# Conditioning sums on the vector engine, and the elementwise engines of the expert loops in program order

## The chip, the core and the metric

The kernel runs on one core of a Trainium2 chip. The metric is the device time of one launch in microseconds (us). The five engines of the core run side by side and each takes its instructions in order: TensorE (PE, with its weight loads as PEld), VectorE (DVE), ScalarE (ACT), GpSimd (POOL) and SyncE (SP), which issues most of the DMA loads.

## What is computed

A two-layer diffusion transformer with mixture-of-experts layers, batch 1, in f32: 256 image tokens `x` and 256 context tokens `xc`, width 1024. Cut to what matters here:

```python
def adaln(cond, w_ada, b_ada):                       # six vectors of 1024 per stream and layer
    m = jax.nn.silu(cond) @ w_ada + b_ada
    return jnp.split(m[..., None, :], 6, axis=-1)

def hybrid_layer(x, xc, c, c_ctx, ..., update_ctx):
    sh1, sc1, gt1, sh2, sc2, gt2 = adaln(c, w_ada, b_ada)               # first stream
    sh1c, sc1c, gt1c, sh2c, sc2c, gt2c = adaln(c_ctx, w_ada, b_ada)     # second stream
    h = modulate(rmsnorm(x, g_mix), sh1, sc1)
    hc = modulate(rmsnorm(xc, g_mix), sh1c, sc1c)
    ...                                              # w_in, rotary, retention, gating, w_pa, w_pb, w_out
    x = x + gt1 * token_mix(h @ w_in, ...)
    ...                                              # the same for xc in layer 0 only
    y = hier_moe(...)                                # 32 experts, top 2, silu(x@w1)*(x@w3) @ w2
    x = x + gt2 * y[:256];  xc = xc + gt2c * y[256:]
```

Layer 0 updates both token sets (512 tokens through its experts). Layer 1 updates the image tokens alone (256).

## The kernel before

**Stages.** By the trace, layer 0's token mixing runs from 0 to about 580 us, layer 0's experts to about 1087, layer 1's mixing to about 1420, layer 1's experts to about 1895, and the final norm ends the span at 1905.3. The weights of all 32 experts are streamed in both layers.

**Mixing.** A weight piece of 512 KB is loaded (`raw`), rounded by ACT (L206, `whi`), and DVE subtracts to get the rest (L207, `wlo`). PE then multiplies three times (L245, L246, L247), which makes an f32 product of rounded parts. For each of four heads, q and k are projected, DVE makes two rotary products for each of them (L808 to L810), POOL adds them (L811), ACT rounds the sum (L320), and POOL subtracts (L321). PE's score matmuls (L245 `mm<-u,u`) want the rounded k.

**Conditioning.** `ada_steps(l, v)` makes vector `v` of layer `l` in eight steps, each with one 512 KB unit of `w_ada`. DVE multiplies the unit by a per-partition scalar and adds it to the first stream's sum (L400, a `scalar_tensor_tensor` of 128x1024). For the second stream, ACT scales the unit (L402) and POOL adds it to the sum (L403). Layer 1's vectors 2 to 5 have only the first stream. The steps are a list, `background`. PE's program calls `tick()` at each block of its work; the test there lets a step be put into the program at three of four ticks in layer 0 and at every tick in layer 1. Vectors (0,2) to (0,5), (1,0) and (1,1) are planned for layer 0, and (1,2) to (1,5) for layer 1. After the last step, `finish` sums over partitions on PE and adds the bias on DVE, and POOL sends the vector to memory.

**Order.** PE and SP run their programs as written (L72). DVE, ACT and POOL are ordered by a scheduler, but for regions where `manual_schedule(engines=ENG3)` fixes them to the program's order: the start, the `routing` region from the last mixing pieces on (L895, closed in `after_turn` at the second expert), and the `between` region from one layer to the next.

**Experts.** One expert is `expert(...)`: matmuls with w1 and w3 (L1240), Silu on ACT (L1243), a product on DVE (L1244), four transposes on PE (L1249), a copy of them by ACT (L1251, `hTt`), and the w2 matmuls (L1257). Around them stand side jobs: `quad_block` gathers tokens for the next four experts on PE (L1204), copied by ACT (L1208) every second block; `combine_parts` has small reduces on DVE (L1229); `gated` multiplies on DVE (L1281) and adds on POOL (L1282).

Of the kernel before, what the change touches and what calls it, by code (L numbers as in the profile page):

```python
# [51 lines left out]
def hybrid_kernel(  # L52
# [162 lines left out]
    def tick():  # L215
        ticks[0] += 1
        while deferred and deferred[0][0] <= ticks[0]:
            deferred.pop(0)[1]()
        if background and (layer[0] or ticks[0] % 4):
            background.pop(0)()  # L220
# [162 lines left out]
    def ada_steps(l, v):  # L383
# [4 lines left out]
        def step(k):  # L388
            raw = raws.pop(0)
            if nexts:  # L390
                raws.append(ada_raw(*nexts.pop(0), u4t if ticks[0] < 30 else a4t))
            for i in range(streams):
                if k == 0:
                    acc.append((u4t if ticks[0] < 24 else a4t)((P, 4, 256)))
                if k == 0 and i:
                    S.activation(acc[i], raw, AF.Copy, scale=cst[:, k, i:i + 1])
                elif k == 0:
                    V.tensor_scalar(out=acc[i], in0=raw, scalar1=cst[:, k, i:i + 1], scalar2=None, op0=ALU.mult)
                elif i == 0:
                    V.scalar_tensor_tensor(out=acc[i], in0=raw, scalar=cst[:, k, i:i + 1], in1=acc[i], op0=ALU.mult, op1=ALU.add)  # L400
                else:
                    S.activation(raw, raw, AF.Copy, scale=cst[:, k, i:i + 1])  # L402
                    G.tensor_tensor(out=acc[i], in0=raw, in1=acc[i], op=ALU.add)  # L403
            if k == KD - 1:
                b = ada_bias(l, v)
                defer(2 if ticks[0] < 24 else 1, lambda: finish(b))
# [22 lines left out]
        def columns(r):  # L429
# [5 lines left out]
            if v == 3:  # L435
                defer(1, lambda: router_const(l))
# [17 lines left out]
    ada_planned([(0, v) for v in range(2, 6)] + [(1, 0), (1, 1)])  # L454
# [79 lines left out]
    for l in range(depth):  # L534
# [117 lines left out]
        else:  # L652
# [35 lines left out]
            def ada_rest():  # L688
                ada_planned([(1, v) for v in range(2, 6)])
                raws.append(ada_raw(*nexts.pop(0), a4t))  # L690

            defer(15, ada_rest)
        fj = [(f, hx, 0, nq) for f in range(2)]
# [693 lines left out]
        for e in range(EXPERTS):  # L1387
# [35 lines left out]
            def after_turn(e=e, pr=pr, e2=e2, q=q, e4=e4, half=half, more=more, more4=more4):  # L1423
                if e == 1:
# [3 lines left out]
                    routing.close()  # L1428
# [7 lines left out]
                if not last and e == EXPERTS - 1:  # L1436
                    between.enter_context(tc.manual_schedule(engines=ENG3))
# [28 lines left out]
        if last:  # L1466
            gfin = u4t()
            nc.sync.dma_start(gfin, g_final.partition_broadcast(P))
# [131 lines left out]
```

## Time and profile before

| | |
|---|---|
| median of 3 runs | 1906.25 us (1904.4 to 1906.83) |
| profiled execution | 1907.06 us, of it span 1905.3 us |
| mean granted TensorE clock | 0.981 |
| PE busy | 1808.8 us (95%) |
| DVE, ACT, POOL busy | 911.3 (48%), 630.9 (33%), 529.5 (28%) |
| DMA | 553.48 MB, mean 290 GB/s |

The span is the time from the first to the last instruction; 1.76 us lie around it. PE is busy in nearly all of the span, so time is won or lost only where PE waits, or where its clock is granted at half, or where the loads set the pace of PE. A granted clock of 1.00 is 2.4 GHz and 0.50 is 1.2 GHz.

### The profile page before, as it was taken

To read this page: it belongs to the slowest core of one execution; us is meant where nothing else is said; L and a number is where in the kernel's file an instruction comes from. 1 tells how busy PE (TensorE), PEld (TensorE's weight loads), DVE (VectorE), ACT (ScalarE), POOL (GpSimd) and SP (SyncE) were. 2 spreads that over 40 slices of the span, in tenths; PEclk is the share of its full clock that TensorE was granted. 3 is DMA by queue.
4 is the path that set the end of the run, shared out by engine and by line. 5 is a ranking of instruction groups with operands and counts; after the bars stand their busy time and mean duration, and the time that the engine had idled before them with its cause. 6 is when DMAs were issued, how large, how long until landed. Compare 5 with 4: busy or idle time off the path is not lost. (4 is left out here: it accounts for less than half of the span.)

```text
span 1905.3 us, 28120 instructions
## 1 busy us (share of the span) xinstructions
PE 1808.8 (95%) x10899; PEld 1239.2 (65%) x10899; DVE 911.3 (48%) x1558; ACT 630.9 (33%) x1013; POOL 529.5 (28%) x416
## 2 busy tenths in 40 slices
PE   6999998899998999999999799999989999999996
PEld 5988898798884444444454399999974444444442
DVE  4878575664644323232333378885553222222223
ACT  3635454444333221222121264444432222222222
POOL 1444354432021424242424342132021122122121
PEclk9999998899998999999999999999999999999998
DMA  9445343344777999999999559863798999999995
GB/s 347 126 171 180 128 154 114 100 160 150 205 232 261 394 404 406 404 400 403 407 402 381 195 165 324 273 199 122 231 351 337 409 409 408 409 409 409 409 409 226
DMA packets 234109, 553.48 MB, mean 290 GB/s; under 512 B 23121, under 2 KB 118513, under 8 KB 233970
## 3 DMA queue, kind: packets, MB, share of 16 engines
q1 hardware_dynamic: 233586, 551.57, 77.9%
q8 instruction: 88, 1.44, 0.3%
q14 instruction: 51, 0.42, 0.1%
q0 software_dynamic: 384, 0.05, 0.0%
HBM read 550.45 MB, written 1.10 MB: 289 GB/s over the span
## 5 line engine op out<-in xcount | busy, mean ns | idle before, releaser
L1282 POOL TENSOR_TENSOR u<-u,t 128x512 f32<-128x512 f32 x184 | 236.0, 1319 | 722.8 <-DVE t L1281 722.8
L1240 PE MATMUL mm<-u,a 128*64 128x512 f32 x1376 | 333.6, 592 | 1.9 <-ACT a L1155 1.4
L207 DVE TENSOR_TENSOR wlo<-raw,whi 128x1024 fp32r<-128x1024 f32 x157 | 217.7, 1389 | 154.1 <-ACT whi L206 153.6
L247 PE MATMUL mm<-u,wlo 128*128 128x256 f32 (+1 forms) x800 | 269.5, 337 | 5.4 <-DVE wlo L207 5.4
L245 PE MATMUL mm<-u,whi 128*128 128x256 f32 (+1 forms) x800 | 270.6, 338 | 0.0
L246 PE MATMUL mm<-u,whi 128*128 128x256 f32 (+1 forms) x800 | 268.4, 336 | 0.0
L1267 DVE SCALAR_TENSOR_TENSOR a<-mm,sw,a 64x512 fp32r<-64x512 f32 x128 | 96.0, 750 | 338.5 <-ACT a L1266 338.0
L245 PE MATMUL mm<-whi,u 128*128 128x256 f32 x832 | 240.2, 289 | 1.9 <-ACT u L569 1.5
L247 PE MATMUL mm<-whi,u 128*128 128x256 f32 x832 | 238.0, 286 | 0.7 <-DVE u L571 0.4
L246 PE MATMUL mm<-wlo,u 128*128 128x256 f32 x832 | 237.1, 285 | 0.8 <-DVE wlo L207 0.8
L1240 PEld LDWEIGHTS mm<-u,a 128*64 128x64 f32 x1376 | 106.2, 137 | 196.3 <-issue 177.6
L206 ACT ACTIVATE whi<-raw 128x1024 fp32r<-128x1024 f32 x160 | 169.7, 1063 | 172.3 <-PE mm L246 65.3
L1281 DVE TENSOR_TENSOR t<-mm,u 128x512 f32<-128x512 f32 x190 | 119.5, 676 | 132.4 <-PE mm L1275 131.8
L247 PEld LDWEIGHTS mm<-u,wlo 128*128 128x128 f32 x800 | 152.8, 191 | 22.6 <-DVE wlo L207 7.3
L245 PEld LDWEIGHTS mm<-whi,u 128*128 128x128 f32 x832 | 161.2, 194 | 6.8 <-issue 3.3
L1266 ACT ACTIVATE a<-mm,sw 64x512 fp32r<-64x512 f32 x128 | 87.4, 682 | 232.4 <-PE mm L1257 187.1
L245 PEld LDWEIGHTS mm<-u,whi 128*128 128x128 f32 x800 | 152.9, 191 | 17.4 <-issue 1.6
L247 PEld LDWEIGHTS mm<-whi,u 128*128 128x128 f32 x832 | 161.0, 193 | 2.0 <-DVE u L571 0.6
L246 PEld LDWEIGHTS mm<-u,whi 128*128 128x128 f32 x800 | 152.7, 191 | 14.6
L246 PEld LDWEIGHTS mm<-wlo,u 128*128 128x128 f32 x832 | 161.2, 194 | 1.3 <-DVE wlo L207 1.2
L1257 PE MATMUL mm<-u,t 128*64 128x512 f32 x664 | 155.5, 604 | 5.9 <-ACT t L1251 5.9
L1243 ACT ACTIVATE t<-mm 64x512 f32<-64x512 f32 x64 | 38.1, 595 | 321.6 <-PE mm L1240 321.6
(314 smaller groups left out, 2562.9 us busy)
## 6 DMA issues: line engine op xcount, KB each, us to landing
u<-in_w_dram SPq DMA_DIRECT2D x510, 512.0 KB
raw<-in_w_in_dram SPq DMA_DIRECT2D x96, 512.0 KB
raw<-in_w_dram SPq DMA_DIRECT2D x75, 512.0 KB
whi<-in_w_dram SPq DMA_DIRECT2D x73, 512.0 KB
wlo<-in_w_dram SPq DMA_DIRECT2D x73, 512.0 KB
a<-in_w_ada_dram SPq DMA_DIRECT2D x57, 512.0 KB
u<-in_w_ada_dram SPq DMA_DIRECT2D x39, 512.0 KB
a<-in_w_dram SPq DMA_DIRECT2D x37, 512.0 KB
```

What stands on the lines that cost most here:

```text
L206: S.activation(hi, rv, AF.Copy)
L207: low_by[0].tensor_tensor(out=lo, in0=rv, in1=hi.bitcast(F32), op=ALU.subtract)
L245: T.matmul(out, lhsT=sh, rhs=mh, start=first, stop=False)
L246: T.matmul(out, lhsT=sh, rhs=ml, start=False, stop=False)
L247: return T.matmul(out, lhsT=sl, rhs=mh, start=False, stop=last)
L1240: T.matmul(o[h * 64:(h + 1) * 64, :], lhsT=x[:, s0:s0 + 64], rhs=w(k), start=(k == 0), stop=(k == KD - 1), tile_position=(0, 64 * h))
L1243: S.activation(hh[0:64], o[64:128, :], AF.Silu)
L1257: T.matmul(o[n % banks][n * 64:(n + 1) * 64, :], lhsT=hTt[:, s], rhs=wc(s)[:, n * 512:(n + 1) * 512], start=(s == 0), stop=(s == 3), tile_ ...
L1266: S.activation(dh, src, AF.Copy, scale=w)
L1267: V.scalar_tensor_tensor(out=dl, in0=src, scalar=w, in1=dh.bitcast(F32), op0=ALU.mult, op1=ALU.subtract)
L1281: V.tensor_tensor(out=y, in0=o, in1=g2[t // 2][:, hs], op=ALU.mult)
L1282: eng.tensor_tensor(out=res[t][:, hs], in0=res[t][:, hs], in1=y, op=ALU.add)
```

## The change

There are four edits. The second stream's sum is made by DVE with the same instruction as the first, so L402 and L403 go (42 of each). A step is put in at seven of eight ticks in layer 0 and at every second tick in layer 1. Vectors (1,2) and (1,3) move from layer 1's mixing into layer 0's, with their 16 loads of 512 KB (and layer 1's routing constant, which waits for vector 3, is made at a fixed tick). The `routing` region closes after the last expert and no more after the second, so DVE, ACT and POOL follow the program through both expert loops. PE and SP have as many instructions as before.

```diff
-        if background and (layer[0] or ticks[0] % 4):
+        if background and ticks[0] % (2 if layer[0] else 8):
             background.pop(0)()
...
-                elif i == 0:
+                else:
                     V.scalar_tensor_tensor(out=acc[i], in0=raw, scalar=cst[:, k, i:i + 1], in1=acc[i], op0=ALU.mult, op1=ALU.add)
-                else:
-                    S.activation(raw, raw, AF.Copy, scale=cst[:, k, i:i + 1])
-                    G.tensor_tensor(out=acc[i], in0=raw, in1=acc[i], op=ALU.add)
...
-            if v == 3:
+            if v == 3 and l == 0:
                 defer(1, lambda: router_const(l))
...
-    ada_planned([(0, v) for v in range(2, 6)] + [(1, 0), (1, 1)])
+    ada_planned([(0, v) for v in range(2, 6)] + [(1, v) for v in range(4)])
...
-                ada_planned([(1, v) for v in range(2, 6)])
+                ada_planned([(1, 4), (1, 5)])
...
             defer(15, ada_rest)
+            defer(20, lambda: router_const(1))
...
                     if last:
                         row_everywhere(g2[0])
-                    routing.close()
...
                 if not last and e == EXPERTS - 1:
+                    routing.close()
                     between.enter_context(tc.manual_schedule(engines=ENG3))
...
         if last:
+            routing.close()
             gfin = u4t()
```

Behind the edit the lines have other numbers: L808 is L806, L811 is L809, L872 is L870, L1208 is L1206, L1244 is L1242, L1251 is L1249, L1267 is L1265, L1281 is L1279.

**DVE, the second head of layer 0's mixing.** First before, then now. `wlo` is a weight rest, `mm_2544` and `mm_2545` (now `mm_2537` and `mm_2538`) are the q and k projections.

```order
L207 TENSOR_TENSOR wlo_2549<-raw_2546,whi_2548 128x1024
L207 TENSOR_TENSOR wlo_2579<-raw_2576,whi_2578 128x1024
L808 SCALAR_TENSOR_TENSOR t_405_2626<-mm_2544,u_262_1678 128x256
L809 SCALAR_TENSOR_TENSOR t_405_2626<-mm_2544,u_262_1678 64x256
L810 SCALAR_TENSOR_TENSOR t_405_2626<-mm_2544,u_262_1678 64x256
L400 SCALAR_TENSOR_TENSOR a_371_2333<-a_434_2802,cst,a_371_2333 128x1024
L808 SCALAR_TENSOR_TENSOR t_408_2636<-mm_2545,u_262_1678 128x256
L321 TENSOR_TENSOR u_316_2049<-mm_2606,u_316_2049 128x512
L321 TENSOR_TENSOR u_317_2050<-mm_2613,u_317_2050 128x512
L809 SCALAR_TENSOR_TENSOR t_408_2636<-mm_2545,u_262_1678 64x256
L810 SCALAR_TENSOR_TENSOR t_408_2636<-mm_2545,u_262_1678 64x256
L207 TENSOR_TENSOR wlo_2656<-raw_2653,whi_2655 128x1024
```

```order
L400 SCALAR_TENSOR_TENSOR a_412_2635<-a_444_2815,cst,a_412_2635 128x1024
L400 SCALAR_TENSOR_TENSOR a_413_2637<-a_444_2815,cst,a_413_2637 128x1024
L207 TENSOR_TENSOR wlo_2670<-raw_2667,whi_2669 128x1024
L321 TENSOR_TENSOR u_326_2068<-mm_2606,u_326_2068 128x512
L321 TENSOR_TENSOR u_327_2069<-mm_2613,u_327_2069 128x512
L413 TENSOR_TENSOR t_410_2629<-mm_2620,t_403_2573 128x512
L806 SCALAR_TENSOR_TENSOR t_415_2640<-mm_2537,u_270_1698 128x256
L807 SCALAR_TENSOR_TENSOR t_415_2640<-mm_2537,u_270_1698 64x256
L808 SCALAR_TENSOR_TENSOR t_415_2640<-mm_2537,u_270_1698 64x256
L806 SCALAR_TENSOR_TENSOR t_418_2650<-mm_2538,u_270_1698 128x256
L807 SCALAR_TENSOR_TENSOR t_418_2650<-mm_2538,u_270_1698 64x256
L808 SCALAR_TENSOR_TENSOR t_418_2650<-mm_2538,u_270_1698 64x256
```

Before, k's rotary products stand behind one conditioning step and two L321 subtractions. Now all six stand behind a step of two streams, a third weight rest, the two subtractions and a `finish` (L413), and follow one another.

**POOL at the same place.** The rotary adds are the rows on `t_404` and `t_407` (now `t_414` and `t_417`).

```order
L403 TENSOR_TENSOR a_372_2335<-a_389_2521,a_372_2335 128x1024
L403 TENSOR_TENSOR a_372_2335<-a_403_2620,a_372_2335 128x1024
L403 TENSOR_TENSOR a_372_2335<-a_430_2743,a_372_2335 128x1024
L811 TENSOR_TENSOR t_404_2625<-t_405_2626 128x256
L321 TENSOR_TENSOR u_406_2632<-t_404_2625,u_406_2632 128x512
L403 TENSOR_TENSOR a_372_2335<-a_434_2802,a_372_2335 128x1024
L811 TENSOR_TENSOR t_407_2635<-t_408_2636 128x256
L321 TENSOR_TENSOR u_409_2642<-t_407_2635,u_409_2642 128x512
```

```order
L870 TENSOR_TENSOR u_355_2178<-u_355_2178,u_356_2179 128x256 x2
L186 TENSOR_TENSOR ors_2401<-ors_2401,mhalf 128x2
L870 TENSOR_TENSOR u_355_2178<-u_355_2178,u_356_2179 128x256 x2
L424 DMA ada_112<-t_410_2629 4x256 x2
L809 TENSOR_TENSOR t_414_2639<-t_415_2640 128x256
L321 TENSOR_TENSOR u_416_2646<-t_414_2639,u_416_2646 128x512
L809 TENSOR_TENSOR t_417_2649<-t_418_2650 128x256
L321 TENSOR_TENSOR u_419_2656<-t_417_2649,u_419_2656 128x512
```

The four L403 rows are gone. The second rotary add still stands behind L321 of the first.

**ACT in the layer-0 expert loop, second and third expert of a group of four.** L1208 (now L1206) is the copy of a gathering block, L1251 (now L1249) the copy that the w2 matmuls want.

```order
L1243 ACTIVATE t_1112_6622<-mm_6605 64x512
L1208 ACTIVATE a_1109_6603<-mm_6625 128x512
L1251 ACTIVATE t_1115_6648<-mm_6643 128x256
L1266 ACTIVATE a_1094_6571<-mm_6659,sw_6385 64x512
L1266 ACTIVATE a_1095_6572<-mm_6659,sw_6385 64x512
L1243 ACTIVATE t_1131_6713<-mm_6696 64x512
L1208 ACTIVATE a_1109_6603<-mm_6650 128x512
L1251 ACTIVATE t_1149_6769<-mm_6764 128x256
```

```order
L1241 ACTIVATE t_1137_6655<-mm_6638 64x512
L1206 ACTIVATE a_1134_6636<-mm_6658 128x512
L1249 ACTIVATE t_1140_6681<-mm_6676 128x256
L1264 ACTIVATE a_1119_6604<-mm_6692,sw_6418 64x512
L1264 ACTIVATE a_1120_6605<-mm_6692,sw_6418 64x512
L1241 ACTIVATE t_1156_6746<-mm_6729 64x512
L1249 ACTIVATE t_1174_6802<-mm_6797 128x256
L1206 ACTIVATE a_1134_6636<-mm_6683 128x512
```

For the second expert the order is as it was. For the third, the copy for the w2 matmuls now stands ahead of the block's copy.

**DVE in the layer-1 expert loop, at every second expert.** L1229 (now L1227) are the small reduces, L1244 (now L1242) is the product behind which PE's transposes stand.

```order
L1267 SCALAR_TENSOR_TENSOR a_2856_14856<-mm_14847,sw_14725,a_2856_14856 64x512
L1267 SCALAR_TENSOR_TENSOR a_2857_14857<-mm_14847,sw_14725,a_2857_14857 64x512
L1229 TENSOR_REDUCE sw_14914<-mm_14911 64x1 x3
L1244 TENSOR_TENSOR t_2871_14903<-mm_14886,t_2871_14903 64x512
L1229 TENSOR_REDUCE sw_14914<-mm_14911 64x1
L1110 TENSOR_TENSOR t_2892_14973<-iota,lr_12949 128x256
```

```order
L1265 SCALAR_TENSOR_TENSOR a_2856_14813<-mm_14804,sw_14682,a_2856_14813 64x512
L1265 SCALAR_TENSOR_TENSOR a_2857_14814<-mm_14804,sw_14682,a_2857_14814 64x512
L1242 TENSOR_TENSOR t_2871_14860<-mm_14843,t_2871_14860 64x512
L1227 TENSOR_REDUCE sw_14871<-mm_14868 64x1 x4
L1265 SCALAR_TENSOR_TENSOR a_2856_14813<-mm_14893,sw_14682,a_2856_14813 64x512
L1265 SCALAR_TENSOR_TENSOR a_2857_14814<-mm_14893,sw_14682,a_2857_14814 64x512
```

The product has moved ahead of three reduces.

## Rows read from the trace of the kernel before

**Rows 1.** Of the page, part 2: GB/s moved in each of 40 slices of the span.

```profile
GB/s 347 126 171 180 128 154 114 100 160 150 205 232 261 394 404 406 404 400 403 407 402 381 195 165 324 273 199 122 231 351 337 409 409 408 409 409 409 409 409 226
```

**Rows 2.** Waits of PE, 150 to 420 us: us in total, times, longest us.

```profile
PE mm L245 <- ACT u L320: 13.5, 2, 7.6
```

**Rows 3.** Timeline of POOL, 276 to 297 us: start, us, engine, line, operation.

```profile
278.87 9.66 POOL L403 TENSOR_TENSOR a<-a,a 128x1024 f32<-128x1024 f32 x3 [0.38 <-ACT a L402]
...
291.40 2.33 POOL L403 TENSOR_TENSOR a<-a,a 128x1024 f32<-128x1024 f32 x1
293.70 0.71 POOL L811 TENSOR_TENSOR t<-t 128x256 f32<-128x256 f32 x1
```

**Rows 4.** Timeline of POOL, 336 to 350 us.

```profile
343.18 3.32 POOL L403 TENSOR_TENSOR a<-a,a 128x1024 f32<-128x1024 f32 x1
346.46 1.70 POOL L811 TENSOR_TENSOR t<-t 128x256 f32<-128x256 f32 x1
```

**Rows 5.** Timeline of DVE, 276 to 297 us, then 336 to 350 us.

```profile
288.26 0.42 DVE L810 SCALAR_TENSOR_TENSOR t<-mm,u 64x256 f32<-64x256 f32 x1
...
341.40 0.42 DVE L810 SCALAR_TENSOR_TENSOR t<-mm,u 64x256 f32<-64x256 f32 x1
```

**Rows 6.** Stretches: us, PE PEld DVE ACT POOL busy (count), PEclk, DMA share, GB/s.

```profile
295.00:302.00 7.00, 6.32 (x29) 6.03 (x30) 4.19 (x7) 2.78 (x5) 1.59 (x2) 0.53 0.19 60
...
349.00:357.00 8.00, 7.45 (x36) 7.15 (x37) 4.26 (x8) 3.14 (x5) 3.50 (x2) 0.55 0.18 61
```

**Rows 7.** Groups of DVE, 50 to 480 us: busy us, mean ns, idle before.

```profile
L207 DVE TENSOR_TENSOR wlo<-raw,whi 128x1024 fp32r<-128x1024 f32 x64 | 98.4, 1543 | 77.3 <-ACT whi L206 77.1
L400 DVE SCALAR_TENSOR_TENSOR u<-u,cst,u 128x1024 f32<-128x1024 f32 x20 | 40.1, 2005 | 0.1
```

**Rows 8.** Lines 400 and 207 over the span: ns min/median/max.

```profile
L400 DVE SCALAR_TENSOR_TENSOR a<-a,cst,a x49: 1245/1278/2308, 252.4 to 1274.3; 128x1024 f32<-128x1024 f32 x49
...
L207 DVE TENSOR_TENSOR wlo<-raw,whi x157: 1198/1225/3420, 23.5 to 1403.5; 128x1024 fp32r<-128x1024 f32 x157
```

**Rows 9.** Stretches of layer-0 mixing, the first and their sum.

```profile
50.00:100.00 50.00, 49.59 (x350) 46.56 (x350) 44.17 (x64) 28.33 (x44) 21.38 (x9) 1.00 0.42 131
...
sum 500.00, PE 484.48 PEld 431.99 DVE 324.54 ACT 222.30 POOL 188.50; mean PE 96.89 PEld 86.40 DVE 64.91 ACT 44.46 POOL 37.70
```

**Rows 10.** Stretches of layer-1 mixing.

```profile
1150.00:1200.00 50.00, 47.84 (x388) 45.76 (x387) 41.90 (x46) 21.31 (x29) 8.53 (x9) 1.00 1.02 364
1205.00:1215.00 10.00, 7.54 (x53) 7.33 (x52) 9.26 (x12) 3.55 (x5) 2.43 (x2) 0.83 0.79 271
```

**Rows 11.** Waits of PE, 1105 to 1400 us (layer-1 mixing).

```profile
PE mm L247 <- DVE wlo L207: 5.4, 7, 2.5
```

**Rows 12.** Waits of PE, 590 to 1060 us (layer-0 experts).

```profile
PE mm L1257 <- ACT t L1251: 7.9, 9, 1.0
```

**Rows 13.** Timeline of ACT, 812 to 820 us.

```profile
816.12 0.60 ACT L1208 ACTIVATE a<-mm 128x512 f32<-128x512 f32 x1 [4.75 <-PE mm L1204]
816.61 0.38 ACT L1251 ACTIVATE t<-mm 128x256 f32<-128x256 f32 x1
```

**Rows 14.** Timeline of PE, 812 to 818.2 us.

```profile
814.47 0.46 PE L1249 MATMUL mm<-ident,t 64*128 64x64 f32 x4
814.86 1.22 PE L1204 MATMUL mm<-a,u 128*128 128x256 f32 x8
817.04 1.08 PE L1257 MATMUL mm<-wlo,t 128*64 128x512 f32 x4 [0.96 <-ACT t L1251]
```

**Rows 15.** Waits of PE, 1400 to 1906 us (layer-1 experts and end).

```profile
PE mm L1249 <- DVE t L1244: 6.0, 15, 1.5
```

**Rows 16.** Timeline of DVE, 1646 to 1658 us.

```profile
1654.56 0.49 DVE L1229 TENSOR_REDUCE sw<-mm 64x1 f32<-64x2 f32 x3 [4.32 <-PE mm L1225]
1655.09 0.68 DVE L1244 TENSOR_TENSOR t<-mm,t 64x512 f32<-64x512 f32 x1
```

**Rows 17.** DMA, 1840 to 1900 us: GB/s in 40 slices of 1.5 us.

```profile
GB/s 410 412 407 412 410 410 412 407 407 412 404 404 410 407 412 410 410 412 407 410 410 407 412 410 407 412 300 249 79 3 0 11 0 0 5 0 5 0 0 19
```

## The prediction

> **What bounds the kernel now.** I read the busy shares first: PE works in 95% of the span, so nothing that another engine saves counts unless PE waits for it. The view to read is therefore PE's waits, taken stage by stage, and then the granted clock behind each longer wait. Four places in them are touched by the change. In layer 0's mixing two waits for a rounded k (ACT L320) take 13.5 us [rows 2]. In layer 1's mixing seven waits for a weight rest take 5.4 us [rows 11]. In layer 0's expert loop the w2 matmuls wait nine times for ACT's copy, 7.9 us [rows 12]. In layer 1's loop, and the few microseconds behind it, the transposes wait 15 times for DVE's product, 6.0 us [rows 15]. The loads are the second thing to read: 400 to 407 GB/s in layer 0's loop and 408 to 409 in most of layer 1's [rows 1]. In layer 1's loop the loads keep that pace until 1879 us and have stopped by about 1885 [rows 17], so there PE can only catch up with them.
>
> **The two long waits in layer 0's mixing.** ACT's copy has its operand from POOL's rotary add, and POOL is in arrears with the second stream's sums. In the second head three L403 adds take 9.66 us, and a fourth of 2.33 us stands between the two rotary adds, so that the second rotary add starts at 293.70 us [rows 3]. DVE had its operand ready at 288.68 (288.26 and 0.42) [rows 5]. In the third head an add of 3.32 us puts the rotary add at 346.46 [rows 4], with the operand ready at 341.82 [rows 5]. So 5.0 and 4.6 us of the 13.5 are plainly POOL's arrears. After each wait PE has a granted clock near half: 0.53 over 7 us and 0.55 over 8 us [rows 6], which costs 7 x 0.47 = 3.3 and 8 x 0.45 = 3.6 us. All that could come back is 13.5 + 6.9 = 20.4 us. The change takes the L403 adds away and also puts more in front of the rotary products on DVE: in the second head, a step's second sum, a third weight rest, two subtractions and a bias add now stand ahead of all six products. Two of those operations alone are 1.28 + 1.22 us [rows 8]. So I leave 3 us of wait in the second head, 2 in the third, and half of the clock's loss (3.4). That gives 20.4 - 5 - 3.4 = **12 us won**. The ends are 20.4 (no wait left) and 0 (DVE is as late as POOL was).
>
> **The extra work on DVE.** 42 sums are moved from ACT and POOL to DVE, and 16 steps of one stream each come over from layer 1: 58 operations, taken at 1.28 us each [rows 8], are 74 us. Some comes back. DVE's own instructions are stretched there, which I put down to POOL's adds beside them: 64 weight rests have a mean of 1543 ns between 50 and 480 us [rows 7] against a median of 1225 [rows 8], 20 us in all, and 20 first-stream sums have 2005 [rows 7] against 1278, 15 us. So DVE's 324.5 us in the 500 us of layer 0's mixing [rows 9] become some 324.5 + 74 - 35 = 364 us, 73%. Two stretches show what that does. Between 50 and 100 us DVE is at 44.2 of 50 and PE loses 0.4 us [rows 9]. In layer 1, at 41.9 of 50, PE loses 2.2 in 50 us [rows 10]. I take **3 us lost** in all, for late weight rests and for the end of the mixing, where ten of the sums, a `finish` and their loads enter a stretch that had none. The ends are 0 and, if all 500 us lost as 1150 to 1200 us did, 22.
>
> The Trainium skill's page "GPSIMD Engine Reference" (Specifications) says that GpSimd's SBUF interfaces are shared with VectorE and contended by its instructions with two SBUF inputs, which the moved sums are. That speaks against the change, since POOL keeps its rotary adds and subtractions; the 2005 ns mean beside POOL's adds [rows 7] agrees. If by that rule all 58 took 2.0 us, DVE would have 42 us more (81%), and with a loss of 7 us in place of 3 the forecast would be 1888 us.
>
> **Layer 1's mixing** loses 16 of its 32 steps, 16 x 1.28 = 20 us of DVE's work, and 8.4 MB of loads. Its seven waits are for weight rests that DVE makes late [rows 11]. The longest is followed by a lower clock: 0.83 over 10 us, 1.7 us lost [rows 10]. With every second tick free of a step I expect about half of 5.4 + 1.7: **3.5 us won**, with ends at 0 and 7.1.
>
> **Layer 0's expert loop.** In the third expert of each group of four, ACT's copy L1251 stands behind the block's copy L1208, which waits for eight matmuls of L1204. The transposes that L1251 wants start at 814.47 and end about 814.93, the L1204 matmuls go on until 816.08, and PE stands still from then to 817.04 [rows 14], because L1208 goes at 816.12 and L1251 only at 816.61 [rows 13]. Seven of the nine waits are of this kind, one for each group that gathers for a next one (7 x 0.96 = 6.7 of the 7.9). Behind the change L1251 stands first, its operand is there 1.1 us before PE is done with L1204, and the copy takes 0.38 [rows 13]. The wait goes, 0.96 us each. What is late next is the loads: they go at 400 to 407 GB/s, and layer 1's steady 409 [rows 1] leaves little. Four experts are 48 units of 512 KB, 25.2 MB: 62.4 us at 403 GB/s and 61.5 at 409, so 0.9 us can go for each group. That gives 7 x 0.9 = **6 us won**, less if the loads already bind. The ends are 0 and 7.
>
> **Layer 1's expert loop.** At odd experts DVE does three small reduces (0.49 us in all) before the product, and the product ends at 1655.77, after PE has run out of the matmuls that cover it [rows 16]. Now the product comes first, and about 0.4 us at each of 15 places goes. But the loads pace this loop, and what counts at the end is only how far behind the last load PE is. I take **4 us won** of 6.0 [rows 15], with ends at 0 and 6.
>
> **The rest** costs nothing that I can see: ACT and POOL have spare time everywhere once L403 is gone, PE's and SP's instructions are as many as before, and the seam between the layers was in program order already.
>
> **The sum** goes against the profiled execution, 1907.06 us (span 1905.3), which is 0.8 above the median. 12 + 6 + 3.5 + 4 - 3 = 22.5 us. 1906.25 - 22.5 = **1884 us**, with a range of its own from 1877 to 1891.
>
> **Rivals.**
> - *DVE takes POOL's place at the heads.* The rotary products stand behind so much that the two waits stay as long as they were. For it: k's three products, which stood behind one sum and two subtractions, now stand behind five operations and q's three products. Against it: 9.7 and 3.3 us of POOL's work go. Without the 12 us: 1896.
> - *The order in the loops is worth nothing, because the loads bind.* For it: 400 to 407 of 409 GB/s [rows 1]. Against it: the loads wait for buffers that PE frees, and a rate that repeats in each group with the same gap looks like PE's pace. Without the 6 and 4 us: 1894.
> - *Both at once:* 1906, which is no change that a measurement can tell (0.2% is about what it can tell, some 3.8 us).
> - *Everything comes back:* 20.4 + 7 + 7.1 + 6 and no loss: 40 us, 1866.
> - *Slower: DVE becomes the bound of layer 0's mixing.* A step of two streams is 2.56 us in front of the next weight rest, in program positions that PE's program sets. Where a rest comes late, PE waits 0.8 us on average (5.4 over 7) [rows 11], and if it waits long, at half clock behind. There are 64 steps. If the heads keep their waits and every second step costs 0.8 us, 32 x 0.8 = 26 us are lost against 13.5 won elsewhere: 1919. It decides from 17 such steps on. Against it: at 88% busy, 50 to 100 us, PE hardly waits [rows 9].
>
> **How the numbers follow.** The forecast as it stands has a chance of 0.42, the heads' rival 0.16, the loops' 0.14, both at once 0.06, everything 0.14, slower 0.08. Faster is 0.42 + 0.16 + 0.14 + 0.14 = 0.86, within 0.2% 0.06, slower 0.08. A range from 1868 to 1900 holds the forecast and the two rivals that win less, and reaches most of the way to the one that wins all. It leaves out the slower case, both at once and the far end of the best.
>
> **What would show it.** *Heads:* PE's waits for L320 fall from 13.5 to about 5 us, with at most one stretch of half clock near 290 and 345 us. If they stay, the rotary add's operand will be seen to come late from DVE. *DVE:* weight rests near their 1225 ns median, about 112 sums of 128x1024, 73% busy up to 550 us, and waits for `wlo` in layer 0 below 4 us. *Layer 1's mixing:* waits for `wlo` near 3 us. *Layer 0's loop:* the seven waits of 0.96 us gone, a group of four at 61.5 to 61.7 us, and loads at 408 or 409. If the group stays at 62.4 with the waits moved to loads, the second rival holds. *Layer 1's loop:* waits for L1242 below 2 us, and the last weights landing less ahead of their matmuls. The forecast is wrong above all if the heads' waits are unchanged, or if new waits for weight rests show between 50 and 560 us.

## The result

The changed kernel takes 1881.5 us (median of four runs, 1879.8 to 1883.6) where the kernel before took 1905.6 (1904.4 to 1906.8) on the same chip: a ratio of 0.9868, 95% interval 0.9856 to 0.9880, or 24 us. A second set on another chip gave 0.9843 (0.9829 to 0.9856). The forecast was 1884 us, with a range from 1868 to 1900. The profiled execution has a span of 1881.7 us. Lines of the changed kernel have the numbers of the changed file.

The page of the changed kernel: busy time of PE, and the granted clock and the GB/s in 40 slices.

```profile
PE 1809.9 (96%) x10899; PEld 1239.5 (66%) x10899; DVE 921.3 (49%) x1600; ACT 585.1 (31%) x969; POOL 416.8 (22%) x374
...
PEclk9999998999999999999999899999999999999998
...
GB/s 352 157 152 190 146 152 118 158 180 222 213 247 257 406 409 408 409 408 409 408 408 399 168 172 282 218 146 132 242 374 317 409 408 409 409 409 408 409 409 238
```

PE is busy for as long as before (1809.9 against 1808.8 us); what went is its idle time. The mean granted clock is 0.981 in both profiled executions: where a stretch of lower clock went, others came. Layer 0's expert loop now loads at 406 to 409 GB/s where it stood at 400 to 407 [rows 1].

PE's waits by stage (us in total, times, longest us): layer 0's mixing (150 to 420 us), layer 0's experts (580 to 1045), layer 1's mixing (1085 to 1380), and layer 1's experts with the end (1380 to 1882).

```profile
PE mm L245 <- ACT u L320: 5.1, 1, 5.1
```

```profile
PE mm L1247 <- DVE t L1242: 2.0, 2, 1.5
PE mm L1255 <- ACT t L1249: 0.5, 1, 0.5
```

```profile
PE mm L247 <- DVE wlo L207: 1.4, 3, 0.6
```

```profile
PE mm L1273 <- DVEq L1473: 2.6, 1, 2.6
PE mm L1247 <- DVE t L1242: 1.4, 1, 1.4
...
PE mm L1238 <- DMA u<-in_w_dram: 1.2, 2, 0.6
```

Of the 13.5 us in layer 0's heads [rows 2] one wait of 5.1 us is left. Of the 7.9 in layer 0's loop [rows 12] 0.5 are left, of the 5.4 in layer 1's mixing [rows 11] 1.4, and of the 6.0 in layer 1's loop [rows 15] 1.4. But in layer 1's loop PE now waits for weights, which it did not before, and the wait ahead of the last matmuls is 2.6 us, where it was 1.5.

To see where the 24 us are, I cut each trace at five marks on PE: the first matmul of layer 0's routing, the transposes of the 30th of layer 0's 32 experts, the first matmul of layer 1, the first matmul of layer 1's routing, and the last L1275 matmuls (L1273 where lines moved). The stages between them, in us of one profiled execution each (the seam, from one layer to the next, holds layer 0's last two experts):

| kernel | mixing, layer 0 | experts, layer 0 | seam | mixing, layer 1 | experts, layer 1 | rest |
|---|---|---|---|---|---|---|
| before | 575.8 | 473.2 | 47.6 | 323.8 | 470.8 | 14.1 |
| changed | 566.6 | 465.3 | 46.8 | 315.8 | 473.0 | 14.2 |
| changed, second set | 564.9 | 465.3 | 50.0 | 314.2 | 470.8 | 14.0 |
| order_only | 575.2 | 465.3 | 48.2 | 323.5 | 469.4 | 14.1 |
| no_order | 565.8 | 473.2 | 49.6 | 316.6 | 473.5 | 14.1 |
| order_l0 | 563.4 | 465.3 | 50.2 | 317.0 | 473.3 | 14.2 |
| dve_sums_only | 565.2 | 473.2 | 46.2 | 322.3 | 473.1 | 13.8 |
| old_sums | 580.3 | 465.3 | 46.8 | 314.6 | 470.8 | 14.1 |
| old_vectors | 562.2 | 465.6 | 46.8 | 322.9 | 471.0 | 13.5 |
| two_ahead | 562.5 | 465.3 | 50.1 | 314.8 | 470.8 | 13.3 |
| phase4_two | 562.3 | 465.3 | 48.4 | 314.0 | 471.5 | 14.1 |
| phase4_two, second set | 558.8 | 465.3 | 48.4 | 314.2 | 472.2 | 13.4 |
| phase4 | 560.5 | 465.6 | 46.8 | 317.0 | 468.9 | 14.1 |
| fewer_loads | 564.9 | 465.3 | 50.2 | 313.4 | 467.9 | 14.2 |

Between the first two rows, 9.2 us were won in layer 0's mixing, 7.9 in its expert loop, 0.8 at the seam and 8.0 in layer 1's mixing, and 2.2 were lost in layer 1's loop. The seam varies from 46.2 to 50.2 us, and by 3.2 between two executions of the changed kernel, so nothing is read from it. Layer 0's loop repeats to 0.3 us, the other stages only to some 2 to 4. The profiled execution of the changed kernel was the slowest of its set both times, that of phase4 the fastest of its five. Times of different sets come from different chips, on which the kernel before took 1906.9, 1908.6 and 1908.0 us; they are compared by their ratio to it.

### The profile page after: what moved, and what is told of

The parts are those of the page before. It is cut to its first block, busy times and chain, and to the rows that moved or that the text cites. A ratio compares the mean times of both kernels' runs of the same rounds, so it can differ in the third digit from the quotient of the medians.

```text
span 1881.7 us, 28055 instructions
## 1 busy us (share of the span) xinstructions
PE 1809.9 (96%) x10899; PEld 1239.5 (66%) x10899; DVE 921.3 (49%) x1600; ACT 585.1 (31%) x969; POOL 416.8 (22%) x374
## 5 line engine op out<-in xcount | busy, mean ns | idle before, releaser
L1280 POOL TENSOR_TENSOR u<-u,t 128x512 f32<-128x512 f32 x184 | 229.5, 1283 | 720.5 <-DVE t L1279 720.5
L1265 DVE SCALAR_TENSOR_TENSOR a<-mm,sw,a 64x512 fp32r<-64x512 f32 x128 | 96.0, 750 | 365.2 <-ACT a L1264 365.1
L207 DVE TENSOR_TENSOR wlo<-raw,whi 128x1024 fp32r<-128x1024 f32 x157 | 198.8, 1266 | 139.9 <-ACT whi L206 139.3
L1242 DVE TENSOR_TENSOR t<-mm,t 64x512 f32<-64x512 f32 x64 | 43.7, 683 | 277.4 <-ACT t L1241 277.4
```

What stands on the lines that cost most here:

```text
L207: low_by[0].tensor_tensor(out=lo, in0=rv, in1=hi.bitcast(F32), op=ALU.subtract)
L1242: V.tensor_tensor(out=hh[0:64], in0=o[0:64, :], in1=hh[0:64], op=ALU.mult)
L1265: V.scalar_tensor_tensor(out=dl, in0=src, scalar=w, in1=dh.bitcast(F32), op0=ALU.mult, op1=ALU.subtract)
L1280: eng.tensor_tensor(out=res[t][:, hs], in0=res[t][:, hs], in1=y, op=ALU.add)
```

## The experiments

### Which edit won which stage

**order_only** is the kernel before with the order edit alone.

```diff
                     if last:
                         row_everywhere(g2[0])
-                    routing.close()
...
                 if not last and e == EXPERTS - 1:
+                    routing.close()
...
         if last:
+            routing.close()
             gfin = u4t()
```

> The kernel before with one edit: the region in program order closes after the last expert, not after the second. Theory A (in layer 1's expert loop the loads set the end, so PE's shorter waits there are eaten by waits for weights): layer 0's loop wins about 7.5 us as in the changed kernel (the seven 0.96 us waits gone), layer 1's loop at most 1.5, so 1905.6 - 8.5 = 1897 us (1895 to 1899), and PE waits for DMA near the end of layer 1's loop. Rival B (PE sets the end of both loops): 7.5 + 6 us won, 1892 us (1890 to 1894), and no waits for weights there.

Measured: 1897.0 us, ratio 0.9946 (0.9929 to 0.9962), 10 us won. Layer 0's loop goes from 473.2 to 465.3. PE's waits from 1390 us on (lines are one higher here than before):

```profile
PE mm L1275 <- DVEq L1475: 2.5, 1, 2.5
PE mm L1240 <- DMA u<-in_w_dram: 2.2, 4, 0.7
PE mm L1249 <- DVE t L1244: 1.4, 1, 1.4
```

DVE's product makes PE wait 1.4 us instead of 6.0 [rows 15]. Instead PE waits 2.2 us for weights, and 2.5 us in front of its last matmuls, where it was 1.5. The stage is only 1.4 us shorter. Theory A's time came out, and so did its waits for DMA.

**no_order** is the changed kernel with this edit undone (the three `routing.close()` as before).

> The changed kernel with one edit undone: the region in program order closes after the second expert again. Theory A (loads set the end of layer 1's loop): layer 0's seven waits of 0.96 us are back, 7.5 us, and at most 1 us of the 15 small waits in layer 1: 1881.5 + 8 = 1889.5 us (1888 to 1891.5). Rival B (PE sets the end of both loops): 1881.5 + 13.5 = 1895 us (1893 to 1897).

Measured: 1891.9 us, ratio 0.9918 (0.9901 to 0.9934), 9 to 14 us slower than the changed kernel's two ratios. Layer 0's loop is back at 473.2 us, with its waits (layer 0's experts):

```profile
PE mm L1255 <- ACT t L1249: 7.9, 9, 1.0
```

So 7.9 us belong to the order in layer 0's loop: it takes 473.2 us in the three kernels with the old order there and 465.3 to 465.6 in the eleven executions with the new. The time lies between the ranges of the two theories and settles neither.

**dve_sums_only** is the kernel before with the second stream's sums on DVE and nothing else.

```diff
-                elif i == 0:
+                else:
                     V.scalar_tensor_tensor(out=acc[i], in0=raw, scalar=cst[:, k, i:i + 1], in1=acc[i], op0=ALU.mult, op1=ALU.add)
-                else:
-                    S.activation(raw, raw, AF.Copy, scale=cst[:, k, i:i + 1])
-                    G.tensor_tensor(out=acc[i], in0=raw, in1=acc[i], op=ALU.add)
```

> The kernel before with one edit: the second stream's sums go to DVE; rate, vectors and loops as before. Theory A (POOL's arrears made both head waits, and in this order DVE makes the rotary products ahead of the step): the waits of PE for L320 fall from 13.5 to under 3 us and the half clock behind them goes, 17 to 20 us won, and DVE's 54 us more against some 35 us of stretching that goes cost at most 3: 1888 us (1885 to 1892). Rival B (DVE takes POOL's place at the heads): at least one wait of 4 us or more stays with its half clock, 1895 to 1902 us.

Measured: 1895.5 us, ratio 0.9938 (0.9921 to 0.9954), 11.5 us won. PE's waits from 150 to 430 us:

```profile
PE mm L245 <- ACT u L320: 4.6, 1, 4.6
PE mm L247 <- POOL u L321: 2.6, 2, 1.8
```

Theory A missed by 7 us. The second head has no wait for L320 and only 1.8 us for POOL's subtraction, and the third head, whose wait is gone in the changed kernel, has 4.6 us. Rival B's time and its one wait above 4 us came out. But it is not DVE that takes POOL's place there, as rival B had it. DVE behind the third head's products, and POOL:

```profile
333.51 0.42 DVE L807 SCALAR_TENSOR_TENSOR t<-mm,u 64x256 f32<-64x256 f32 x1
333.96 3.48 DVE L400 SCALAR_TENSOR_TENSOR a<-a,cst,a 128x1024 f32<-128x1024 f32 x2
```

```profile
334.06 2.30 POOL L321 TENSOR_TENSOR u<-t,u 128x512 fp32r<-128x512 f32 x1 [0.74 <-ACT u L320]
336.33 1.70 POOL L808 TENSOR_TENSOR t<-t 128x256 f32<-128x256 f32 x1
```

DVE's last rotary product ends at 333.93, before PE runs out of other work at 334.10. POOL then makes q's subtraction ahead of k's add, as its order says, and takes 2.30 and 1.70 us for them beside two sums on DVE; in the changed kernel's second head (below) the same two take 1.26 and 0.72 us with DVE idle beside most of them. So here the wait is POOL's order and POOL's slower work.

**old_sums** is the changed kernel with ACT and POOL making the second stream's sums again, at the denser rate.

> The changed kernel with one edit undone: ACT scales and POOL adds the second stream again, at the new, denser rate. Theory A (these sums are what keeps POOL in arrears): both head waits are there, 13 us or more, each with its half clock: 1881.5 + 8 + 3.5 = 1893 us (1889 to 1899). Rival B (the rate and the moved vectors made the gain in layer 0): 1882 us (1880 to 1885) with one wait as in the changed kernel.

Measured: 1893.2 us, ratio 0.9932 (0.9911 to 0.9953), the time that theory A has, and layer 0's mixing is 580.3 us, longer than before the change. But the waits are not the two that theory A rests on, so its time came out by luck in part (150 to 430 us, then two rows of DVE):

```profile
PE mm L245 <- DVE t L831: 5.9, 2, 4.5
PE mm L245 <- ACT u L320: 5.1, 1, 5.1
```

```profile
260.68 3.42 DVE L400 SCALAR_TENSOR_TENSOR a<-a,cst,a 128x1024 f32<-128x1024 f32 x1
...
267.49 2.83 DVE L321 TENSOR_TENSOR u<-t,u 128x512 fp32r<-128x512 f32 x1
```

One is at a head, 5.1 us, as in the changed kernel itself. Another of 4.5 us is in the retention of a head, for a DVE result (L831), with smaller ones for POOL's subtraction (2.3 us) and a weight rest (1.1). In front of that result DVE's sum takes 3.42 us, against a median of 1.28 [rows 8], and its subtraction 2.83, against a mean of 0.68 in the changed kernel, while POOL adds the second stream (259.6 to 269.8 us). The rate and the moved vectors without the move to DVE lengthen layer 0's mixing by 4.5 us, in one execution each.

**old_vectors** is the changed kernel with vectors (1,2) and (1,3) made in layer 1's mixing again, at every tick.

```diff
-        if background and ticks[0] % (2 if layer[0] else 8):
+        if background and (layer[0] or ticks[0] % 8):
...
-    ada_planned([(0, v) for v in range(2, 6)] + [(1, v) for v in range(4)])
+    ada_planned([(0, v) for v in range(2, 6)] + [(1, 0), (1, 1)])
...
-                ada_planned([(1, 4), (1, 5)])
+                ada_planned([(1, v) for v in range(2, 6)])
```

> The changed kernel with one edit undone: vectors 2 and 3 of layer 1 are made in layer 1's mixing again, with a step at every tick there. Theory A (16 steps and 8.4 MB in layer 1's mixing made the late weight rests): PE's waits for wlo there are back at 5 us with one long wait and its half clock, 7 us lost, and about 2 us of PE work for the two vectors' ends moves from layer 0 to layer 1: 1888 us (1886 to 1890). Rival B (the waits there fell for another reason, as the second stream's place or the order): 1881.5 us (1880 to 1883).

Measured: 1884.8 us, ratio 0.9883 (0.9868 to 0.9898). The time lies between the ranges of the two theories. PE's waits in layer 1's mixing:

```profile
PE mm L247 <- DVE wlo L207: 5.4, 7, 2.5
```

They are exactly those of before [rows 11], and the stage is 322.9 us again. Layer 0's mixing is 562.2 us, 2.7 to 4.4 less than in the two traces of the changed kernel. So the waits are theory A's: the move wins 7 to 9 us in layer 1 and costs 3 to 4 in layer 0. By the ratios, 0.9883 against 0.9868 and 0.9843, it is worth 3 or 8 us; the interval of the first set overlaps this one, that of the second does not. The other two gains add up: dve_sums_only and order_only won 11.5 and 10 us each alone, and this kernel, which has both, some 22 by its ratio.

### The wait that was left at the second head

The changed kernel's DVE from 280 to 294 us, and POOL behind it.

```profile
285.61 2.48 DVE L400 SCALAR_TENSOR_TENSOR a<-a,cst,a 128x1024 f32<-128x1024 f32 x2 [3.44 <-DMA a<-in_w_ada_dram]
288.00 1.22 DVE L207 TENSOR_TENSOR wlo<-raw,whi 128x1024 fp32r<-128x1024 f32 x1
289.14 1.28 DVE L321 TENSOR_TENSOR u<-mm,u 128x512 fp32r<-128x512 f32 x2
290.34 0.68 DVE L413 TENSOR_TENSOR t<-mm,t 128x512 f32<-128x512 f32 x1
290.94 0.41 DVE L806 SCALAR_TENSOR_TENSOR t<-mm,u 128x256 f32<-128x256 f32 x1
...
293.13 0.42 DVE L808 SCALAR_TENSOR_TENSOR t<-mm,u 64x256 f32<-64x256 f32 x1
```

```profile
291.31 1.20 POOL L424 DMA_DIRECT2D ada<-t  x2 [12.56 <-DVE t L413]
292.54 0.73 POOL L809 TENSOR_TENSOR t<-t 128x256 f32<-128x256 f32 x1
294.01 1.26 POOL L321 TENSOR_TENSOR u<-t,u 128x512 fp32r<-128x512 f32 x1 [0.74 <-ACT u L320]
295.23 0.72 POOL L809 TENSOR_TENSOR t<-t 128x256 f32<-128x256 f32 x1
```

DVE stands 3.44 us for a unit of conditioning weights, with two sums, a weight rest, two subtractions and a bias add ahead of the rotary products in its queue. These start at 290.94 and end at 293.55. POOL first sends out the vector (L424, 1.20 us) and then adds, waits for ACT, subtracts, and adds again until 295.95. This second add, k's, has its operand at 293.55 and stands 1.7 us behind q's subtraction. PE starts its scores at 296.67, after 5.1 us. Before, POOL was the late one: its second add started at 293.70 with operands from 288.68 [rows 3, 5].

**two_ahead** takes the load's part away.

```diff
-            raws.append(ada_raw(*nexts.pop(0)))
+            raws.extend(ada_raw(*nexts.pop(0)) for _ in range(2))
```

> The changed kernel with one edit: two units of the conditioning weights are loaded ahead of the step that uses them, not one. Theory A (at the second head DVE's queue is held 3.4 us by a step whose load has not landed, and the rotary products stand behind it): that wait of DVE goes, PE's wait for L320 falls from 5.1 to 1.5 to 2.5 us and some of the half clock behind it goes, 3 to 5 us won: 1877.5 us (1875.5 to 1879). Rival B (the amount of DVE work in front of the products makes the wait, load or not): the wait stays over 4 us and the time at 1881 (1879.5 to 1883).

Measured: 1879.6 us, ratio 0.9855 (0.9840 to 0.9870), not to be told from the changed kernel's. DVE's sums of that step and the first rotary product, then PE's wait for k:

```profile
282.08 2.48 DVE L400 SCALAR_TENSOR_TENSOR a<-a,cst,a 128x1024 f32<-128x1024 f32 x2 [1.52 <-DMA a<-in_w_ada_dram]
...
287.41 0.41 DVE L806 SCALAR_TENSOR_TENSOR t<-mm,u 128x256 f32<-128x256 f32 x1
```

```profile
PE mm L245 <- ACT u L320: 3.2, 1, 3.2
```

DVE stands 1.52 us where it stood 3.44, and PE 3.2 us instead of 5.1: both fell by 1.9. That is less than A expected, because the load is still late, and because what is behind DVE stays: from DVE's last product to PE's first score matmul it takes 3.1 us in both kernels, with k's add 1.7 us behind q's subtraction on POOL.

**phase4_two** also moves the tick without a step, from the eighth of eight to the fourth (the expectations count it as the fifth), and **phase4** does that alone.

```diff
-        if background and ticks[0] % (2 if layer[0] else 8):
+        if background and (ticks[0] % 2 if layer[0] else ticks[0] % 8 != 4):
```

> The changed kernel with two edits: two units loaded ahead, and the tick without a step is the fifth of eight instead of the eighth, which takes a weight rest, two subtractions and a bias add from in front of the second head's rotary products and leaves one step's second sum between them. Theory A (what stands in front of the products on DVE makes the wait): PE's wait for L320 under 1 us in all heads, no half clock there: 1881.5 - 4.5 - 3 = 1874 us (1872 to 1877). Rival B (a new place takes over, as an added step of two sums elsewhere): 1879 to 1884.

> The changed kernel with the free tick moved to the fifth of eight alone, one unit loaded ahead as in the changed kernel. Theory A (at the second head the load and the order both hold the products): a step's second sum still stands between q's and k's products and waits for its load, so half of the gain: 1.5 to 3 us below after_again. Rival B (only the order matters): as phase4_two_again. Rival C (only the load matters): as after_again.

> The same kernel as phase4_two. Theory A (the second head's wait was worth some 4 us, with its half clock): 3 to 5 us below after_again, 0.9845 of the kernel before. Rival B (the difference between the earlier ratios, 0.9868 and 0.9845, was between chips): within 1.5 us of after_again.

> The changed kernel as it is, on the chip of the three others of this set, to compare with them. Both theories: 0.987 of the kernel before (0.9855 to 0.988).

Measured (the changed kernel itself came out below the range expected of it): phase4_two 1878.7 us, 0.9845 (0.9832 to 0.9859), and in the second set 1874.3, 0.9835 (0.9820 to 0.9850); phase4 1877.7, 0.9850 (0.9837 to 0.9864); the changed kernel beside them 1877.2, 0.9843 (0.9829 to 0.9856). PE's waits of phase4_two from 150 to 430 us in the second set, and two stretches around the second head (PEclk is the number behind POOL's):

```profile
PE mm L247 <- POOL u L321: 1.8, 1, 1.8
PE mm L245 <- DVE t L828: 1.6, 2, 0.9
```

```profile
285.00:295.00 10.00, 8.18 (x74) 7.26 (x73) 9.88 (x12) 4.68 (x8) 6.03 (x4) 1.00 0.26 76
295.00:302.00 7.00, 7.00 (x61) 7.00 (x60) 7.00 (x14) 4.33 (x8) 1.20 (x2) 1.00 0.66 214
```

There is no wait for L320 any more and no lower clock behind the head. Layer 0's mixing is 562.3 and 558.8 us, where the changed kernel has 566.6 and 564.9. So the wait is gone in the trace, and the stage is 4 to 6 us shorter. In time, phase4_two is 2.9 us below the changed kernel beside it, just short of theory A's 3 to 5, with intervals that overlap, and it missed the 1874 us of its first expectation by 5. It beats the kernel before clearly; that it beats the changed kernel is not shown by its time.

phase4, with the free tick alone, has no wait for L320 either. A row of its DVE and one of its POOL:

```profile
283.82 1.28 DVE L400 SCALAR_TENSOR_TENSOR a<-a,cst,a 128x1024 f32<-128x1024 f32 x1 [3.06 <-DMA a<-in_w_ada_dram]
```

```profile
289.67 3.50 POOL L321 TENSOR_TENSOR u<-t,u 128x512 fp32r<-128x512 f32 x2
```

DVE still stands 3.06 us for a load right in front of the rotary products, and that costs PE no such wait now: the weight rest, the subtractions and the bias add have moved behind the products (k's end at 288.84), and POOL's order has changed too, with both adds ahead of the two subtractions. So a late load makes the wait longer, as two_ahead shows, and the order of the work, on DVE and on POOL, makes it or takes it away. How much of this is DVE's order and how much POOL's is not shown. phase4's mixing is 560.5 us, as short as with both edits, but its median time is not below the changed kernel's; what it is worth in time stays open.

### What sets the end of layer 1's experts

**fewer_loads** takes away 24 of the loads of layer 1's experts: from the ninth expert on, the last quarter of w2 is not loaded, and the third is used in its place.

```diff
             e, i = divmod(j, 12)
             c = i % 4
+            if l and e >= 8 and i == 11:
+                units.append(units[-1])
+                continue
```

> The changed kernel with part of layer 1's expert loads taken away: from the ninth expert of layer 1 on the last quarter of w2 is not loaded, and the third quarter is used in its place (24 loads of 512 KB, 12.6 MB, 30.8 us at 409 GB/s). All instructions of PE, DVE, ACT and POOL stay. Theory A (the loads set the end of layer 1's loop in the changed kernel): PE's waits for DMA are gone and what PE had won by 1829 us stays won, about 5 us: 1876.5 us (1874 to 1879), and no more than that, since PE is then the bound. Rival B (PE sets the end): 1881.5 us (1880 to 1883).

Measured: 1877.8 us, ratio 0.9847 (0.9832 to 0.9862), which lies between the changed kernel's two ratios, so the time does not tell the theories apart. The stage does: it is 467.9 us, the shortest of all. Two stretches of it (the last number is GB/s):

```profile
1700.00:1800.00 100.00, 100.00 (x526) 47.03 (x526) 26.82 (x54) 22.52 (x40) 19.15 (x16) 1.00 1.03 408
1800.00:1850.00 50.00, 49.47 (x250) 21.46 (x250) 13.80 (x24) 10.58 (x18) 9.92 (x8) 1.00 0.58 219
```

PE waits for no weights any more. The loads, still at 408 to 409 GB/s up to 1800 us, are over early: 219 in the last stretch. So the loads cost this stage 1 to 5 us (468.9 to 473.0 in the other kernels with the new order; some 3 us against those whose clock was alike, see order_l0), and 467.9 is about what PE needs.

They cost it at its end alone. Over most of the loop the transposes of every second expert are 28.49 us apart with the new order, the same in fewer_loads as in the changed kernel, and 28.85 in order_l0 and in the kernel before. The 24 loads of two experts take 30.8 us at 409 GB/s. So PE is faster than the loads and lives on weights that were loaded ahead, until they are used up: from the 30th expert's transposes to the last one's it is 30.07 us in the changed kernel (second set) and 26.97 in fewer_loads.

**order_l0** keeps the new order in layer 0's loop alone.

```diff
                     if last:
                         row_everywhere(g2[0])
+                        routing.close()
...
         if last:
-            routing.close()
             gfin = u4t()
```

> The changed kernel with the region in program order closed after the second expert in layer 1, as before, and after the last one in layer 0, as now. Theory A (layer 1's loop is set by its loads, so that its order is worth nothing): within 1 us of after_again, with PE's 15 waits for DVE's product back (6 us) and its waits for DMA gone. Rival B (the order there wins some of its 6 us): 2 to 6 us above after_again.

Measured: 1883.8 us, ratio 0.9873 (0.9858 to 0.9888), 6.6 us above the changed kernel beside it (0.9843, 0.9829 to 0.9856). PE's waits from 1385 us on, first of order_l0, then of the changed kernel in the same set:

```profile
PE mm L1247 <- DVE t L1242: 6.0, 15, 1.5
...
PE mm L1273 <- ACTq L1473: 1.5, 1, 1.5
```

```profile
PE mm L1273 <- DVEq L1473: 2.6, 1, 2.6
PE mm L1238 <- DMA u<-in_w_dram: 1.4, 3, 0.6
PE mm L1247 <- DVE t L1242: 1.4, 1, 1.4
```

The waits are as theory A has them, but its time is not: the order in layer 1's loop is worth something. Between the two profiled executions lie 4.2 us: 2.6 in layer 1's loop (473.3 against 470.8), 2.8 in layer 1's mixing, and some 1 us the other way in the rest. In layer 1's mixing the two kernels run the same program; there 1.0 us is a longer wait for POOL at 1375 us, and a lower clock follows it (0.83 over 1372 to 1382 us, against 1.00).

The clock also has to be alike where the loop is compared, since the kernels differ in the mean clock over its first 20 us. At 0.87 to 0.89 and full clock behind, the old order took 470.8 us (before) and the new 469.4 and 468.9 (order_only, phase4). At 0.74 to 0.76, the old order took 473.1 to 473.5 (no_order, dve_sums_only, order_l0) and the new 470.8 to 471.5 (the changed kernel's second set, old_sums, phase4_two). So the order is worth some 1.4 to 2.7 us.

Counting bytes says the same. I set the bytes of all loads issued up to the last expert weight against the bytes that had landed. The last weight lands 460 to 464 us behind the stage's start in all kernels of the table but fewer_loads, whatever the order. With the old order PE's last matmuls start 10.4 to 11.0 us after that (before, no_order, dve_sums_only, order_l0), with the new one 7.2 to 9.7 (nine executions). So the loads set the end of the stage, and the order decides how closely PE follows them: some 2 us, against 6.0 of waits that went.

## Why the prediction was right, and where it was not

**The sum** was 22.5 us, and 24.1 were measured; the range held it. Its parts did less well than their sum: that 8.0 us in place of 3.5 in layer 1's mixing stand against a loss in place of 4 in layer 1's loop is luck.

**The heads: 12 forecast, 12.0 measured, by other parts.** I left 3 us of wait in the second head, 2 in the third, and half of the clock's loss. Instead the third head's 7.6 us went whole with their 3.6 us of lower clock (the granted clock is 1.00 from 304 to 560 us), and of the second head's 5.9 only 0.8 went: 5.1 stayed, at a granted clock of 0.53 over 293 to 304 us, where it was 0.53 over 295 to 302 [rows 6]. That the two sums agree is luck. The step that failed is the second head. I took DVE's queue there by the length of its instructions, 1.28 and 1.22 us, and not by what they wait for: a step's sum waits for its load (3.44 us), and what stands behind it waits too. I also put POOL's own order at nothing, and it holds k's add 1.7 us behind q's subtraction. At that head the rival "DVE takes POOL's place" was right in the main. two_ahead shows that the load is part of the wait, phase4 and phase4_two that the wait goes when the order changes, and dve_sums_only that POOL can still hold a head without the second stream's sums.

**DVE's extra work: 3 lost in the forecast, about 3 measured (12.0 at the heads less the stage's 9.2), for another reason.** DVE's time from 50 to 550 us (the sum of five stretches; DVE's is the third number):

```profile
sum 500.00, PE 492.07 PEld 437.61 DVE 356.22 ACT 178.10 POOL 91.88; mean PE 98.41 PEld 87.52 DVE 71.24 ACT 35.62 POOL 18.38
```

It is 356 us, or 71%, for a forecast of 364 (73%). Late weight rests cost nothing new in layer 0. What was lost is PE's own work for the two moved vectors, which I had put at nothing since PE's instructions are as many as before. They are, but 16 matmuls of L409, two of L430 and their company came over from layer 1, some 2 us. A longer stretch of lower clock comes to that (below). dve_sums_only, with no vector moved, won 10.6 us in this stage.

**Layer 1's mixing: 3.5 forecast, 8.0 measured.** The mechanism was right and the term too small. I expected half of the 7.1 us of waits and lower clock to go. 4.0 us of those waits went (one of 1.0 us for POOL came in this execution, not in the second set's), and all of the 1.7 behind the long one, since the long one went. The PE work that left for layer 0, some 2 us, is most of the rest. old_vectors brings back the same seven waits and 7 to 9 us.

**Layer 0's loop: 6 forecast, 7.9 measured.** Seven waits of 0.96 us went, and each group of four experts is 1.03 us shorter. The limit that I had put on them, the loads' 409 GB/s, is now reached, and it was a little further off than I had it: four experts took 62.57 us and not 62.4 (the time from one of the seven waits to the next), and now take 61.54, which is 25.2 MB at 409 GB/s. PE still waits for no weights there, and 61.54 is about what is left of 62.57 without the wait, so the pace is still PE's own. 0.7 us more came from a wait of 0.6 at 1037 us.

**Layer 1's loop: 4 forecast, 2.2 lost in the profiled execution, about 2 won over all runs.** The step took the share that the loads leave to be two thirds of 6.0. They leave less, some 2 us, as order_l0 and the landing of the last weight show. That the profiled execution lost here goes with a lower clock at 1427 to 1434 and 1860 to 1864 us, which the execution before did not have. Rival two, "the loads bind", was wrong for layer 0 and mostly right for layer 1. How the 6.6 us between the medians of order_l0 and the changed kernel divide beyond that stays open.

**The Trainium skill's sentence** on GpSimd's shared interfaces, in the page "GPSIMD Engine Reference" (Specifications), would have given 1888 us if all moved sums had run at 2.0 us. They have a median of 1278 ns as before, and the longest is 2352. With POOL's busy time down by 113 us there was less to contend with. Where the two engines do meet, both take longer: POOL's 2.30 and 1.70 us in dve_sums_only, DVE's 3.42 and 2.83 in old_sums.

## What to carry to other kernels

An engine that takes its work in order delays what stands behind a waiting instruction, so work that is put on it in the background is priced by what it waits for, and by what is queued behind it, not by its length alone. When a queue in arrears is emptied, look who feeds the same consumer next: here DVE's queue was the next to hold the rotary products, and behind it the order of what was left on POOL. Where loads set the end of a loop, a shorter chain in it is worth only how much closer the last work follows the last load. And stages of two executions are compared at like granted clock.

## What was not expected of the hardware

The granted clock fell to half without any wait of PE. Three stretches of the changed kernel (PE's busy time is the second number, PEclk stands behind POOL's) and PE's timeline around the first and ahead of the last:

```profile
186.00:197.00 11.00, 11.00 (x48) 9.33 (x48) 6.40 (x10) 1.90 (x3) 0.00 (x0) 0.69 0.45 163
293.00:304.00 11.00, 6.58 (x29) 6.29 (x30) 7.56 (x10) 4.37 (x7) 3.68 (x4) 0.53 0.10 34
...
1427.00:1434.00 7.00, 7.00 (x22) 3.08 (x22) 5.26 (x27) 1.44 (x3) 0.00 (x0) 0.51 1.03 400
```

```profile
185.75 3.31 PE L460 MATMUL mm<-wr,mod 128*128 128x36 f32 x24
...
194.90 0.39 PE L247 MATMUL mm<-u,wlo 128*128 128x512 f32 x1
```

```profile
1425.49 2.33 PE L479 MATMUL mm<-u,ones 1*128 1x512 f32 x4
```

From 186 to 197 us PE is busy for all 11.00 us, at a mean clock of 0.69, and from 1427 to 1434 for all 7.00, at 0.51. Ahead of the first stand 24 matmuls of 36 columns (L460) in 3.31 us, and the 512-column ones behind them take 0.63 us each until 194.5 and 0.39 to 0.40 after 194.9. Ahead of the second are four matmuls with one row of input (L479). Before, the same matmuls had a lower clock for a shorter time (0.79 over 204 to 212 us) and a full one at the second place (1.00 over 1449 to 1460). So the clock fell there as it falls behind a wait, and at the same cost, but not in every execution: the changed kernel's second set has a full clock behind the same L479 matmuls (1.00 over 1414 to 1444 us). Both falls came behind small matmuls; that these are the cause is not shown.
